# Hybrid attention and pooling block: pooled-branch loads and latents moved earlier, last output product in two halves

## The chip, the cores and the metric

The kernel runs on one core of a Trainium2 chip. The metric is device microseconds of one execution. A core has TensorE (PE in the profile, its weight loads PEld), VectorE (DVE), ScalarE (ACT), GpSimd (POOL) and SyncE (SP), each with a queue of its own that it works through in order. SP issues nearly all transfers of this kernel.

## The reference

One layer over 1024 tokens of width 1024. One input projection makes the latents of attention, two SiLU gates, the input of a pooling branch and the merge gates. Both branches are gated, projected and merged; an output projection, a residual add and a normalisation of each row end it.

```python
hn = rms_norm(h, norm_in)
zq, zkv, zkr, g_attn, u_pool, g_pool, g_merge = split(hn @ w_in)
y_attn = mla_attention(zq, zkv, zkr, ...) * silu(g_attn)     # 8 heads, chunk-causal
y_pool = multiscale_pool(u_pool, ...) * silu(g_pool)         # windows 2, 4, 8, 16
a = y_attn @ w_branch_attn
p = y_pool @ w_branch_pool
gate_a, gate_p = split(sigmoid(g_merge))
h = h + (gate_a * a + gate_p * p) @ w_out
return rms_norm(h, norm_final)
```

## The kernel before

Every fp32 operand is split into a high and a low part (`split`: ACT casts the high part, DVE subtracts it to get the low part), and a product is three matmuls: high by high, high by low, low by high. Tiles are 128 rows high; a matmul writes up to 512 columns of a PSUM bank.

The order of the work is not that of the source. Each helper (`mms`, `act`, `tt`, `dma`, ...) adds an `Op` to a `Plan`. `Plan.order` then schedules all of them with one running time per engine and a modelled cost of each operation: of the operations whose inputs are there, an engine takes the earliest in program order among those that could start within 30 of the first (line 189). Tiles come from tags with a fixed number of slots (`SLOTS`, line 25): 45 slots of `t`, one of `wr` (raw weights), two each of `wh` and `wl` (their high and low parts), two banks pairs `s` (scores) and one bank `f` (products of the pooled branch) among them. The result is one fixed queue for each engine. An instruction whose input is late holds up all that stand behind it in its queue.

The program has these stages.

1. **Input projection**: pairs of column blocks in seven products each instead of eight (`Pair`). `gate_pair(14, ...)` is the last; beside its products 4 and 6 stand the two `Latents` items (line 1148), which load the q and kv latents (`zq`, `zkv`) again, normalise and split them.
2. **Up products** (`run_up`): q and k of all heads from the latents, results written to DRAM by head (`qn_d`, `kn_d`). The first q item also loads the four pooled rows `yp` (`y<-y_d`); each k item splits one of them (lines 830 to 831). `run_rope` makes the rotary part of q. Weights: `w_uq`, `w_uk`, `w_uv`.
3. **Value products** (`run_v`): eight products `pv`, each with a cast on ACT and a subtraction on DVE.
4. **Attention**: eight heads. Head h loads the rows of head h+1 (`load_head`: `qh`, `ql`, `kh`, `kl`), and one tile `mp[h]` of the pooled branch's merge gates (lines 1412 to 1413). Then scores `sc`, their maximum on DVE, the exponential on ACT (`pr`), transposes `pt`, their split `pT`, and the product with the values `o`. Score banks have two slots, so a score waits until the exponential two before it has read its slot.
5. **Pooled-branch products** (`run_branch_p`, eight items of 24 matmuls, `pf`) lie between the matmuls of the heads. Each needs its weights (`wr<-w_bp`, split to `wh` and `wl`) and, at the end of each half, multiplies the bank into `mp[t]`. There is one bank for them, so the next half waits for that multiplication.
6. **Branch items** (`BranchItem`): the attention branch's projection, merge, and the loads of the blocks of `w_out` (`BLOCKS`).
7. **Output projection**: `Ahead` and four `OutPair`s, each with six products of two row tiles; `Rows` adds the products onto the residual rows, squares and sums them, scales by the final norm (`nf`) and by the reciprocal root, and writes out. The pair i = 3 is the last.

Of the kernel before, what the change touches and what calls it, by code (L numbers as in the profile page):

```python
# [209 lines left out]
def hybrid_block_kernel(  # L210
# [30 lines left out]
    def buf(tag, cols, dt, name):  # L241
        uid[0] += 1
        nm = f"{name}_{uid[0]}"
        pool = pp if tag in PSUM else tp
        b = Buf(lambda: pool.tile([P, cols], dt, tag=tag, bufs=SLOTS[tag], name=nm), tag)
        b.nm = name
        return View(b, 0, P, 0, cols)
# [9 lines left out]
    def t32(name):  # L257
        return buf("t", T, F32, name)
# [45 lines left out]
    def tt(o, a, b, op, eng="DVE"):  # L304
        e = nc.vector if eng == "DVE" else nc.gpsimd
        c = 1.055 * a.n + 145 if eng == "DVE" else 2.2 * a.n + 150
        port = eng == "POOL" or not (psum(a) or psum(b))
        plan.add(eng, lambda: e.tensor_tensor(real(o), real(a), real(b), op), c, [a, b], [o], port=port)  # L308
# [16 lines left out]
    def stt(o, a, s, b, op0, op1):  # L325
        c = 1.055 * a.n + 145 + 62 * len(views(s))
        plan.add(
            "DVE",
            lambda: nc.vector.scalar_tensor_tensor(real(o), real(a), real(s), real(b), op0, op1),
            c,  # L330
            views(a, s, b),
            [o],
            port=not (psum(a) or psum(b)),
        )
# [37 lines left out]
    def dma(o, x, late=None):  # L372

        v = o if isinstance(o, View) else x
        p0, p1, c0, c1 = v.box
        plan.add(
            "SP",
            lambda: nc.sync.dma_start(real(o), real(x)),  # L378
            450,
            views(x, late),  # L380
            views(o),
            (p1 - p0) * (c1 - c0) * 4,
        )
# [18 lines left out]
    def split_tile(x):  # L402
        h, l = tr("hi"), tr("lo")
        split(h, l, x)
        return h, l
# [55 lines left out]
    def cell(n=1):  # L461
        a = small_at[0]
        small_at[0] += n
        return small[:, a : a + n]
# [340 lines left out]
    def load_rope(h):  # L805
        d = heads[h % 2]
        j = 32 * (h % 4)
        for x, n in enumerate("hl"):
            dma(d["q" + n][64:96, :].f32(), qr_d[h // 4][x][j : j + 32, :])
# [9 lines left out]
    def run_up(p, which, first):  # L819
        def run(it):  # L820
            acc = next_acc()
            cs = state["cq"] if which == "q" else state["ckv"]
            n = len(cs)
            if first:
                shared[which] = (it.h, it.l)
            if which == "q" and p == 0:
                for g in range(4):
                    yp[g] = t32("y")
                    dma(yp[g], y_d[g])
            if which == "k":  # L830
                yp[p] = split_tile(yp[p])
            if which == "k" and p == 1:
                dress_slots(heads[0])
                load_rope(0)
            wh, wl = shared[which]
            o = n * (p if which == "k" else p % 2)
            prod(acc, wh[o : o + n], wl[o : o + n], halves(cs))
            h, l = tr("uh"), tr("ul")
            for ps, a, b in acc.spans:
                split(h[:, a:b], l[:, a:b], ps)  # L840
            dst = qn_d if which == "q" else kn_d
            if p == 0:
                if which == "q":
                    make_slots()
                dma(heads[0][which + "h"][0:64, :].f32(), h[0:64, :].f32())
                dma(heads[0][which + "l"][0:64, :].f32(), l[0:64, :].f32())
            r = 64 if p == 0 else 0
            dma(dst[p][0][r:P, :], h[r:P, :].f32())
            dma(dst[p][1][r:P, :], l[r:P, :].f32())
        return run  # L850
# [22 lines left out]
    def run_v(j):  # L873
        def run(it):
            if j == 0:
                shared["v"] = (it.h, it.l)
            wh, wl = shared["v"]
            c = "pofp"[j % 4]
            ps = buf(c, 512, F32, "pv")
            sl = slice(128 * j, 128 * j + 128)  # L880
            seq = []
            for k, (ch, cl) in enumerate(state["ckv"]):
                seq += [(ch[:, sl], wh[k]), (ch[:, sl], wl[k]), (cl[:, sl], wh[k])]
            mms([(ps, a, b, n == 0, n == 5) for n, (a, b) in enumerate(seq)])
            v = tr("v")
            v4 = lambda x: v.via(
                lambda a: a.rearrange("p (h x d) -> p h x d", h=HEADS, x=2)[:, :, x, :]
            )
            pv = ps.via(lambda a: a.rearrange("p (h d) -> p h d", h=HEADS))
            acopy(v4(0), pv)  # L890
            tt(v4(1), pv, v4(0).f32(), ALU.subtract)
            vt.append(v)
        return run

    yp = [None] * 4
# [230 lines left out]
    def gate_pair(t, beside=()):  # L1126
        items.append(Pair(14 + t, (spill_sigmoid(gate_d[t]), spill_sigmoid(gate_d[t + 1])), beside))
# [17 lines left out]
    silu_pair(4, ga_d[2:4])  # L1145
    gate_pair(10)
    gate_pair(12, [(3, Rotary())])
    gate_pair(14, [(4, q), (6, kv)])
    for n, it in enumerate(i for i in items if isinstance(i, Pair)):
        for j, f in enumerate(hooks.get(n, [])):  # L1150
            it.after[1 + 3 * j] = f
# [11 lines left out]
    n_pre = len(items)  # L1163

    mp = [None] * 8

    def rows_of(t):
        return m_d[t // 4][128 * (t % 4) : 128 * (t % 4) + 128, :]
# [22 lines left out]

    ys = []

    BLOCKS = ("b11", "b21", "t2", "t1", "t3", "b22", "t4")
    blocks_at = {
        "b11": (w_top, 0),
        "b21": (w_low, 0),
# [5 lines left out]
    class BranchItem(Item):  # L1203
# [7 lines left out]
        def load(self):  # L1211
            super().load()
            self.g = t32("gate")
            dma(self.g, gate_d[self.t])
            self.blocks = []
            for n in BLOCKS[self.t : self.t + 1]:
                src, c = blocks_at[n]
                for j in range(2):
                    raw = t32("wo")
                    k2 = lambda a: a.rearrange("(k p) c -> p k c", p=P)  # L1220
                    x = src[256 * j : 256 * j + 256, c : c + 512]
                    dma(raw.via(lambda a: a.rearrange("p (k c) -> p k c", k=2)), x.via(k2) if isinstance(x, View) else k2(x))
                    self.blocks += [raw[:, lft], raw[:, rgt]]
# [26 lines left out]
    class Rows:  # L1250


        def __init__(self, i):
            self.row = [i, i + 4]
            self.t = [t32("res"), t32("res")]
            self.ss = [cell(2), cell(2)]
            self.st = [cell(), cell()]
            for e in range(2):
                dma(self.t[e], xr[128 * self.row[e] : 128 * self.row[e] + 128, :])

        def add(self, e, h, bank):
            v = self.t[e][:, (lft, rgt)[h]]
            tt(v, bank, v, ALU.add)

        def square(self, e, h):
            act(buf("go", 512, F32, "junk"), self.t[e][:, (lft, rgt)[h]], AF.Square, acc=self.ss[e][:, h : h + 1])
# [4 lines left out]

        def finish(self, e, last=False):
            r, ss, st = self.t[e], self.ss[e], self.st[e]
            tt(st, ss[:, 0:1], ss[:, 1:2], ALU.add)
            act(st, st, AF.Sqrt, scale=1.0 / D, bias=eps)
            recip(st, st)
            o = out[128 * self.row[e] : 128 * self.row[e] + 128, :]
            if last:
                act(r[:, rgt], r[:, rgt], AF.Copy, scale=st)
                stt(r[:, lft], r[:, lft], st, nf[:, lft], ALU.mult, ALU.mult)  # L1280
            else:
                stt(r, r, st, nf, ALU.mult, ALU.mult)
            for c in (lft, rgt):
                dma(o[:, c], r[:, c])
# [32 lines left out]
    class OutPair(Pair):  # L1317
# [30 lines left out]
        def run(self, it, tick):  # L1348
            i, R = self.i, self.rows
            b = first["b"][i]  # L1350
            c = first["c"][i] or buf("of"[i - 2], 512, F32, "pb")
            a = buf("p", 512, F32, "pb")
            tick()
            R.add(0, 0, b)
            self.product(a, 1, True)
            R.add(0, 0, a)
            R.square(0, 0)
            tick()
            self.product(b, 2, False)
            R.add(0, 1, b)  # L1360
            tick()
            self.product(c, 3, True)
            R.add(1, 1, c)
            tick()
            self.product(b, 4, False)
            R.add(1, 1, b)
            R.square(1, 1)
            if i == 3:
                R.scale(1, 1)
            tick()  # L1370
            self.product(c, 5, False)
            R.add(0, 1, c)
            R.square(0, 1)
            R.finish(0)
            tick()
            self.product(b, 6, False)
            R.add(1, 0, b)
            R.square(1, 0)
            R.finish(1, i == 3)

    raw_tag[0] = "t"
    for t in range(8):
# [24 lines left out]
    for h in range(HEADS):  # L1407
        if h + 1 < HEADS:
            load_head(h + 1)
        if 0 < h < 4:  # L1410
            load_gate(h)
        mp[h] = t32("mp")
        dma(mp[h], gate_d[8 + h])
        s = heads[h % 2]
        for qr in range(4):
            prs = []
# [139 lines left out]
```

## Time and profile before

| what | us |
|---|---|
| median of 3 runs | 705.21 (702.76 to 706.47) |
| profiled execution | 705.3 |
| its span | 703.4 |

The profiled execution is 0.1 above the median of the runs, and its span leaves 1.9 around it. PE is busy for 97% of the span. A row of the timeline gives the start of an instruction, its duration, engine, line, operation and tiles, and in brackets how long the engine had been idle before it and what ended that. `sc`, `pf`, `pv`, `pt` and `o` are PSUM tiles of the products named above, `ps` and `pb` those of the input and output projections.

### The profile page before, as it was taken

Reading aid. Unit: us, or ns where it says so; the run is one execution under the profiler, and the core shown is the slowest. Engines: PE = TensorE matmul, PEld = TensorE weight load, DVE = VectorE, ACT = ScalarE, POOL = GpSimd, SP = SyncE. Lnnn points to the kernel's source line nnn. Section 1 sums busy time; section 2 is a strip of 40 time slices with the busy share of each in tenths; the row PEclk is TensorE's granted clock in tenths of the full one; section 3 lists DMA queues with packets and bytes.
Section 4 is the critical chain, followed back from the end, with each engine's and each line's share of the span. In section 5 each row is a group of like instructions: output and inputs, shape, how many; then the busy total and the mean of one; then the engine's idle time right before and its main releaser. Section 6 shows DMA issues by size and latency. Waiting matters only on the chain.

```text
span 703.4 us, 9678 instructions
## 1 busy us (share of the span) xinstructions
PE 681.5 (97%) x3356; PEld 573.3 (82%) x3356; DVE 539.8 (77%) x863; ACT 355.8 (51%) x657; POOL 115.6 (16%) x153
## 2 busy tenths in 40 slices
PE   8999999999999999999998879999999999999995
PEld 6878888888888888888886769999998978878884
DVE  5698996768878577768869548878787899957883
ACT  6854535442444354444436537677666673425431
POOL 0020100400022030400101023445454200000000
PEclk9999999999999999999999989999999999999999
DMA  8956666452977549375687973454441399784522
GB/s 317 377 189 253 210 221 179 99 160 102 308 211 180 179 162 298 101 180 156 243 278 276 332 165 107 110 145 121 106 120 46 108 378 336 227 258 160 187 83 89
DMA packets 55871, 136.42 MB, mean 194 GB/s; under 512 B 5904, under 2 KB 17296, under 8 KB 55696
## 3 DMA queue, kind: packets, MB, share of 16 engines
q1 hardware_dynamic: 53568, 131.63, 56.0%
q0 software_dynamic: 2256, 4.20, 4.3%
q8 instruction: 26, 0.43, 0.3%
q14 instruction: 21, 0.17, 0.1%
HBM read 93.73 MB, written 46.27 MB: 199 GB/s over the span
## 4 chain that ended last, share of the span: by engine, by line
PE 84%; DMA 6%; DVE 5%; ACT 2%; issue 1%; SPq 1%; DVEq 0%; ACTq 0%
PE pb L275 33%; PE ps L275 30%; PE sc L275 6%; PE pf L275 6%; PE o L275 4%; PE pt L282 4%; DMA mp<-gate_d 2%; DMA m_d<-gate 1%; DMA kl<-kr_d 1%; DVE lo L308 1%; DMA wr<-w_uv 1%; DVE ra L308 1%; DVE gate L308 1%; SPq L378 1%; DMA wr<-w_bp 1%
## 5 line engine op out<-in xcount | busy, mean ns | idle before, releaser
L275 PE MATMUL pb<-t,wp 128*128 128x512 f32 x504 | 120.9, 389 | 0.0
L275 PEld LDWEIGHTS pb<-t,wp 128*128 128x128 f32 x504 | 94.6, 188 | 19.6
L298 ACT CAST wp<-wr 128x512 fp32r<-128x512 f32 x98 | 59.4, 620 | 93.3 <-PE ps L275 53.1
L308 DVE TENSOR_TENSOR wp<-wr,wp 128x512 fp32r<-128x512 f32 x98 | 72.0, 748 | 36.8 <-ACT wp L298 35.5
L275 PE MATMUL ps<-xa,wp 128*128 128x512 f32 x224 | 74.0, 390 | 0.0
L322 POOL TENSOR_SCALAR pr<-pr,small 128x384 f32<-128x384 f32 (+4 forms) x64 | 48.2, 759 | 73.8 <-DVE small L348 65.9
L308 DVE TENSOR_TENSOR pT<-pt,pT 128x512 fp32r<-128x512 f32 (+1 forms) x80 | 48.4, 632 | 12.1 <-ACT pT L298 11.8
L290 ACT ACTIVATE pr<-sc,small 128x384 f32<-128x384 f32 (+4 forms) x64 | 47.6, 745 | 18.8 <-DVE small L357 17.7
L298 ACT CAST pT<-pt 128x512 fp32r<-128x512 f32 (+1 forms) x80 | 41.5, 545 | 29.8 <-PE pt L282 29.0
L357 DVE TENSOR_REDUCE small<-sc 128x1 f32<-128x128 f32 (+3 forms) x64 | 47.6, 751 | 10.4 <-PE sc L275 10.0
L275 PEld LDWEIGHTS ps<-xa,wp 128*128 128x128 f32 x224 | 42.0, 188 | 8.7
L275 PE MATMUL o<-pT,v 128*128 128x256 f32 (+1 forms) x320 | 47.8, 281 | 0.2 <-DVE pT L308 0.2
L275 PEld LDWEIGHTS o<-pT,v 128*128 128x128 f32 x320 | 44.4, 189 | 3.3 <-DVE pT L308 0.4
L275 PE MATMUL ps<-xb,wp 128*128 128x512 f32 x112 | 43.6, 389 | 0.0
L282 PE MATMUL pt<-ident,pr 128*128 128x128 f32 x288 | 42.7, 278 | 0.0
L275 PE MATMUL ps<-t,wp 128*128 128x512 f32 x168 | 40.8, 390 | 0.0
L275 PE MATMUL pb<-xa,wp 128*128 128x512 f32 x168 | 40.7, 389 | 0.0
L275 PE MATMUL pb<-wo,wp 128*128 128x512 f32 x168 | 39.9, 389 | 0.0
L275 PE MATMUL sc<-kh,qh 128*128 128x384 f32 (+4 forms) x96 | 36.2, 377 | 2.3 <-ACT pr L290 2.3
L275 PEld LDWEIGHTS pb<-wo,wp 128*128 128x128 f32 x168 | 31.5, 188 | 6.6
L275 PEld LDWEIGHTS pb<-xa,wp 128*128 128x128 f32 x168 | 31.5, 188 | 6.5
L275 PEld LDWEIGHTS ps<-t,wp 128*128 128x128 f32 x168 | 31.4, 188 | 6.5
(206 smaller groups left out, 1444.9 us busy)
## 6 DMA issues: line engine op xcount, KB each, us to landing
wr<-w_z SPq DMA_DIRECT2D x30, 512.0 KB, 5.2
gate_d<-z SPq DMA_DIRECT2D x16, 512.0 KB, 3.4
xt<-xr SPq DMA_DIRECT2D x8, 512.0 KB, 10.5
mp<-gate_d SPq DMA_DIRECT2D x8, 512.0 KB, 5.0
gate<-gate_d SPq DMA_DIRECT2D x8, 512.0 KB, 5.8
wo<-wt_d SPq DMA_DIRECT2D x8, 512.0 KB, 8.7
m_d<-gate SPq DMA_DIRECT2D x16, 256.0 KB, 4.2
mr<-m_d SPq DMA_DIRECT2D x16, 256.0 KB, 4.4
```

The source lines that it names most:

```text
L275: nc.tensor.matmul(real(o), real(a), real(b), start=s, stop=e, **kw)
L282: nc.tensor.transpose(real(o), real(a), real(ident))
L290: nc.scalar.activation(real(o), real(x), func, scale=real(scale), **kw)
L298: lambda: nc.scalar.copy(real(o), real(x)),
L308: plan.add(eng, lambda: e.tensor_tensor(real(o), real(a), real(b), op), c, [a, b], [o], port=port)
L322: e.tensor_scalar(real(o), real(a), real(s1), real(s2), op0, op1)
L357: lambda: nc.vector.tensor_reduce(real(o), real(a), axis=AX.X, op=ALU.max, negate=True),
L378: lambda: nc.sync.dma_start(real(o), real(x)),
```

## The change

Four edits.

- **Gates fetched with the pooled rows.** `mp[0]` is loaded in the first q item, right behind the pooled rows, `mp[1]` in the second k item. Heads 2 to 7 load theirs as before.
- **Latents one product sooner.** They stand beside products 3 and 5 of the last pair instead of 4 and 6.
- **Pooled rows split between value products.** The four `split_tile(yp[p])` move from the four k items to value products 0, 2, 4 and 6.
- **Last product in two halves.** In the last `OutPair`, product 1 (A12 by b21) is computed last, in two banks of 256 columns. The second row tile (e = 1) is finished ahead of it; the first is added, scaled and squared in pieces of 256. A `None` in `BLOCKS` moves the loads of the block `t4` one branch item later.

```diff
-            if which == "k":
-                yp[p] = split_tile(yp[p])
+                load_mp(0)
             if which == "k" and p == 1:
...
+                load_mp(1)
...
             vt.append(v)
+            if j in (0, 2, 4, 6):
+                p = (0, 2, 4, 6).index(j)
+                yp[p] = split_tile(yp[p])
...
-    gate_pair(14, [(4, q), (6, kv)])
+    gate_pair(14, [(3, q), (5, kv)])
...
+    def load_mp(t):
+        mp[t] = t32("mp")
+        dma(mp[t], gate_d[8 + t])
...
-    BLOCKS = ("b11", "b21", "t2", "t1", "t3", "b22", "t4")
+    BLOCKS = ("b11", "b21", "t2", "t1", "t3", "b22", None, "t4")
...
+        def piece(self, bank, n):
+            c = slice(256 * n, 256 * n + 256)
+            v, ss = self.t[0][:, c], self.ss[0]
+            tt(v, bank, v, ALU.add)
+            act(buf("go", 512, F32, "junk")[:, :256], v, AF.Square, acc=ss[:, 2 * n : 2 * n + 1])
+            if n == 0:
+                tt(ss[:, 0:1], ss[:, 0:1], ss[:, 1:2], ALU.add)
+                tt(v, v, nf[:, c], ALU.mult)
...
-            if last:
+            if last and not e:
                 act(r[:, rgt], r[:, rgt], AF.Copy, scale=st)
-                stt(r[:, lft], r[:, lft], st, nf[:, lft], ALU.mult, ALU.mult)
+                stt(r[:, 256:512], r[:, 256:512], st, nf[:, 256:512], ALU.mult, ALU.mult)
+                ts(r[:, :256], r[:, :256], st, None, ALU.mult)
+            elif last:
+                act(r, r, AF.Copy, scale=st)
...
-        mp[h] = t32("mp")
-        dma(mp[h], gate_d[8 + h])
+        if h > 1:
+            load_mp(h)
...
+            R.scale(1, 0)
+            R.finish(1, True)
+            for n in range(2):
+                q = slice(256 * n, 256 * n + 256)
+                a = buf("p", 512, F32, "pb")[:, :256]
+...
+                R.piece(a, n)
+            R.finish(0, True)
```

The queue of ACT in the second half of head 0, before. A number behind a name tells tiles of one name apart; `pr<-sc` are the exponentials of 768 and 896 keys and of head 1's first block.

```order
L298 CAST pT_3403<-pt_3390 128x384
L290 ACTIVATE pr_3317,small<-sc_3374,small 128x768
L290 ACTIVATE pr_3311,small<-sc_3397,small 128x896
L298 COPY oa_3438<-o_3411 64x256
L298 CAST pT_3452<-pt_3440 128x512
L298 CAST pT_3465<-pt_3446 128x512
L290 ACTIVATE pr_3311,small<-sc_3455,small 128x128
L298 CAST pT_3492<-pt_3483 128x384
L290 ACTIVATE pr_3498,small<-sc_3417,small 128x1024
L290 ACTIVATE pr_3317,small<-sc_3494,small 128x256
L298 COPY oa_3516<-o_3477 64x256
L298 CAST wh_3525<-wr_3352 128x512
```

The same stretch of ACT now.

```order
L298 CAST pT_3422<-pt_3403 128x384
L290 ACTIVATE pr_3325,small<-sc_3392,small 128x768
L298 CAST wh_3434<-wr_3359 128x512
L298 COPY oa_3453<-o_3438 64x256
L290 ACTIVATE pr_3323,small<-sc_3418,small 128x896
L298 CAST pT_3476<-pt_3462 128x512
L298 CAST pT_3488<-pt_3468 128x512
L298 CAST pT_3509<-pt_3497 128x384
L290 ACTIVATE pr_3517,small<-sc_3449,small 128x1024
L290 ACTIVATE pr_3323,small<-sc_3479,small 128x128
```

The cast of the third pooled weights (`wh<-wr`, the last row before, the third now) has moved ahead of the copy and the exponential of 896 keys. The weights' load on SP, before, behind the last loads of head 1's rows:

```order
L378 DMA ql_3289<-qn_d_2944 64x1024
L378 DMA kl_3291<-kn_d_3136 64x1024
L378 DMA mp_3309<-gate_d_2255 128x1024
L378 DMA wr_3352<-w_bp 128x512
L378 DMA qh_2916<-qr_d_3001 32x1024
```

The same place of SP now.

```order
L378 DMA kh_3291<-kn_d_3113 64x1024
L378 DMA ql_3293<-qn_d_2962 64x1024
L378 DMA kl_3295<-kn_d_3141 64x1024
L378 DMA wr_3359<-w_bp 128x512
L378 DMA qh_2928<-qr_d_3013 32x1024
```

The load of `mp[0]` is gone from between; it stands 48 places further up, behind the pooled rows. On PE, 15 pooled matmuls `pf` stand ahead of head 1's first score before, and 30 now. On DVE the last rows of the program, before (`res_6104` is the second row tile, `res_6102` the first):

```order
L308 TENSOR_TENSOR res_6102<-pb_6288,res_6102 128x512
L308 TENSOR_TENSOR small<-small 128x1
L348 RECIPROCAL small<-small 128x1
L329 SCALAR_TENSOR_TENSOR res_6102<-res_6102,small,nf_5696 128x1024
L308 TENSOR_TENSOR res_6104<-ps_5837,res_6104 128x512
L308 TENSOR_TENSOR small<-small 128x1
L348 RECIPROCAL small<-small 128x1
L329 SCALAR_TENSOR_TENSOR res_6104<-res_6104,small,nf_5696 128x512
```

The same end of DVE now.

```order
L308 TENSOR_TENSOR res_6104<-ps_5801,res_6104 128x512
L308 TENSOR_TENSOR res_6102<-pb_6189,res_6102 128x256
L308 TENSOR_TENSOR res_6104<-res_6104,nf_5701 128x512
L308 TENSOR_TENSOR small<-small 128x1 x2
L308 TENSOR_TENSOR res_6102<-res_6102,nf_5701 128x256
L348 RECIPROCAL small<-small 128x1
L308 TENSOR_TENSOR res_6102<-pb_6352,res_6102 128x256
L308 TENSOR_TENSOR small<-small 128x1
L348 RECIPROCAL small<-small 128x1
L329 SCALAR_TENSOR_TENSOR res_6102<-res_6102,small,nf_5701 128x256
L320 TENSOR_SCALAR res_6102<-res_6102,small 128x256
```

The wide last operation of the first row tile is gone from the end, the finish of the second stands among the pieces of the first, and the add of the second piece (`pb_6352`) stands behind the reciprocal of the second tile.

## Rows read from the trace of the kernel before

**Rows 1.** The page: busy time of each engine, share of the span, instructions.

```profile
PE 681.5 (97%) x3356; PEld 573.3 (82%) x3356; DVE 539.8 (77%) x863; ACT 355.8 (51%) x657; POOL 115.6 (16%) x153
```

**Rows 2.** Timeline of PE, the idle times between 370 and 420 us.

```profile
373.34 0.73 PE L275 MATMUL ps<-hi,wl 128*128 128x512 f32 x2 [1.37 <-DVE wl L308]
...
385.02 0.50 PE L275 MATMUL pv<-wh,hi 128*128 128x512 f32 x1 [1.41 <-DVE ul L308]
...
403.32 0.41 PE L275 MATMUL sc<-kh,qh 128*128 128x320 f32 x1 [1.48 <-ACT pr L290]
...
415.49 0.80 PE L275 MATMUL pf<-hi,wh 128*128 128x512 f32 x1 [4.87 <-DVE mp L308]
...
418.50 0.46 PE L275 MATMUL sc<-kh,qh 128*128 128x128 f32 x1
```

**Rows 3.** Timeline of ACT, SP and DVE, 400 to 416 us.

```profile
401.70 0.62 ACT L298 CAST wh<-wr 128x512 fp32r<-128x512 f32 x1 [2.65 <-DMA wr<-w_bp]
...
402.35 0.69 DVE L308 TENSOR_TENSOR wl<-wr,wh 128x512 fp32r<-128x512 f32 x1 [1.49 <-ACT wh L298]
...
403.44 0.59 SPq L378 DMA_DIRECT2D kl<-kn_d  x1
...
404.09 0.57 SPq L378 DMA_DIRECT2D mp<-gate_d  x1
...
406.51 0.36 SPq L378 DMA_DIRECT2D wr<-w_bp  x1
...
409.46 1.01 ACT L290 ACTIVATE pr<-sc,small 128x896 f32<-128x896 f32 x1 [1.01 <-DVE small L348]
...
414.74 0.69 DVE L308 TENSOR_TENSOR mp<-pf,mp 128x512 f32<-128x512 f32 x1 [5.30 <-DMA mp<-gate_d]
```

**Rows 4.** Transfers issued from 403.4 to 406.8 us: size, us from issue to landing.

```profile
mp<-gate_d SPq DMA_DIRECT2D x1, 512.0 KB, 10.6
kl<-kn_d SPq DMA_DIRECT2D x1, 256.0 KB, 9.3
wr<-w_bp SPq DMA_DIRECT2D x1, 256.0 KB, 9.5
```

**Rows 5.** Stretches: sum; PE, PEld, DVE, ACT, POOL busy; clock; DMA share, GB/s.

```profile
376.00:410.00 34.00, 30.75 (x151) 25.29 (x150) 25.06 (x40) 20.77 (x39) 5.02 (x8) 1.00 1.01 324
414.45:421.25 6.80, 5.76 (x20) 4.97 (x21) 3.77 (x8) 1.63 (x4) 1.90 (x3) 0.53 0.46 94
421.35:424.00 2.65, 2.65 (x21) 2.48 (x21) 0.95 (x3) 1.58 (x4) 0.09 (x1) 1.00 0.00 0
```

**Rows 6.** Lines by form: count, busy, mean ns; value subtractions and pooled-row subtractions on DVE.

```profile
L308 DVE TENSOR_TENSOR v<-pv,v 128x512 fp32r<-128x512 f32 x8 | 5.3, 685 | 2.5 <-ACT v L298 2.5
...
L308 DVE TENSOR_TENSOR lo<-y,hi 128x1024 fp32r<-128x1024 f32 x4 | 4.9, 1215 | 0.0
```

**Rows 7.** Timeline of the end of the program.

```profile
692.79 2.88 PE L275 MATMUL ps<-wo,wp 128*128 128x512 f32 x12
...
695.26 1.28 DVE L329 SCALAR_TENSOR_TENSOR res<-res,small,nf 128x1024 f32<-128x1024 f32 x1
...
696.46 0.68 DVE L308 TENSOR_TENSOR res<-ps,res 128x512 f32<-128x512 f32 x1
...
697.24 0.63 ACT L290 ACTIVATE junk<-res 128x512 f32<-128x512 f32 x1 [2.21 <-DVE res L308]
...
698.18 0.29 ACT L290 ACTIVATE small<-small,eps 128x1 f32<-128x1 f32 x1 [0.23 <-DVE small L308]
...
698.71 0.72 ACT L290 ACTIVATE res<-res,small 128x512 f32<-128x512 f32 x1 [0.23 <-DVE small L348]
```

**Rows 8.** By form and from PE's timeline: rows nearest to the new shapes.

```profile
L308 DVE TENSOR_TENSOR oa<-o,oa 64x256 f32<-64x256 f32 x32 | 13.4, 419 | 3.5 <-ACT oa L298 3.0
...
L290 ACT ACTIVATE z<-z 128x1024 f32<-128x1024 f32 x16 | 16.7, 1058 | 16.1 <-DVE z L308 16.1
...
553.71 1.14 PE L275 MATMUL o<-pT,v 128*128 128x256 f32 x8
```

More of the change, by code (lines that the diff above doesn't have):

```diff
@@ L1215, in load @@
             self.blocks = []
-            for n in BLOCKS[self.t : self.t + 1]:
+            for n in filter(None, BLOCKS[self.t : self.t + 1]):
                 src, c = blocks_at[n]
@@ L1255, in __init__ @@
             self.t = [t32("res"), t32("res")]
-            self.ss = [cell(2), cell(2)]
+            self.ss = [cell(3), cell(2)]
             self.st = [cell(), cell()]
@@ L1273, in finish @@
             r, ss, st = self.t[e], self.ss[e], self.st[e]
-            tt(st, ss[:, 0:1], ss[:, 1:2], ALU.add)
+            if last and not e:
+                tt(st, ss[:, 0:1], ss[:, 2:3], ALU.add)
+            else:
+                tt(st, ss[:, 0:1], ss[:, 1:2], ALU.add)
             act(st, st, AF.Sqrt, scale=1.0 / D, bias=eps)
@@ L1277, in finish @@
             o = out[128 * self.row[e] : 128 * self.row[e] + 128, :]
-            if last:
+            if last and not e:
                 act(r[:, rgt], r[:, rgt], AF.Copy, scale=st)
-                stt(r[:, lft], r[:, lft], st, nf[:, lft], ALU.mult, ALU.mult)
+                stt(r[:, 256:512], r[:, 256:512], st, nf[:, 256:512], ALU.mult, ALU.mult)
+                ts(r[:, :256], r[:, :256], st, None, ALU.mult)
+            elif last:
+                act(r, r, AF.Copy, scale=st)
             else:
@@ L1351, in run @@
             c = first["c"][i] or buf("of"[i - 2], 512, F32, "pb")
-            a = buf("p", 512, F32, "pb")
+            last = i == 3
             tick()
             R.add(0, 0, b)
[L1355 to L1358, printed above, removed]
+            if not last:
+                a = buf("p", 512, F32, "pb")
+                self.product(a, 1, True)
+                R.add(0, 0, a)
+                R.square(0, 0)
+                tick()
             self.product(b, 2, False)
@@ L1367, in run @@
             R.square(1, 1)
-            if i == 3:
+            if last:
                 R.scale(1, 1)
@@ L1373, in run @@
             R.square(0, 1)
-            R.finish(0)
+            if last:
+                R.scale(0, 1)
+            else:
+                R.finish(0)
             tick()
@@ L1378, in run @@
             R.square(1, 0)
-            R.finish(1, i == 3)
+            if not last:
+                R.finish(1)
+                return
+            R.scale(1, 0)
[3 more added lines that the diff above has]
+                a = buf("p", 512, F32, "pb")[:, :256]
+                for k, ((ah, al), (bh, bl)) in enumerate(zip(self.ops["A12"], W["b21"])):
+                    mms(
+                        [
+                            (a, ah, bh[:, q], k == 0, False),
+                            (a, ah, bl[:, q], False, False),
+                            (a, al, bh[:, q], False, k == 3),
+                        ]
+                    )
+                R.piece(a, n)
+            R.finish(0, True)
     raw_tag[0] = "t"
```

## The prediction

> **What bounds the kernel now.** The page's first part comes first: PE is busy for 681.5 of 703.4 us, DVE for 539.8 [rows 1]. What can be won on PE is the time in which it stands, the time at the lower clock, and the tail. So I next read PE's timeline for idle times. Around the places of the change it stands four times: 1.37 at 373.3 and 1.41 at 385.0, both for DVE's low parts, 1.48 at 403.3 for an exponential, 4.87 at 415.5 for DVE's multiplication into `mp` [rows 2]. The timeline of the other engines says why. DVE waited 5.30 for the gate tile, issued at 404.09; ACT stood 2.65 for the second pooled weights, ahead of the exponential for which PE stood 1.48 [rows 3]. The transfers say why those are late: the gate tile lands 10.6 after its issue, at 414.7, and from 376 to 410 the DMA engines are busy all the time (share 1.01) [rows 4, 5]. Transfers land in the order of issue: head 1's last rows at 403.44 + 9.3 = 412.7, the gates at 414.7, the third pooled weights at 406.51 + 9.5 = 416.0 [rows 3, 4]. The long wait costs twice: from 414.45 to 421.25 the granted clock is 0.53 (1.2 of 2.4 GHz), and 5.76 us of PE work lie there, which lose 0.47 x 5.76 = 2.7; behind, it is 1.00 again [rows 5].
>
> **Loads of the gates.** The wait for `mp` goes: tile 0 is now issued behind the pooled rows, tile 1 in the k items, long before their use. What is late next stands in the queue of ACT: the cast of the third pooled weights has moved ahead of the exponential of 896 keys, which in the profile ran at 409.46 without waiting for a transfer [rows 3]. Head 1's first score needs the bank that this exponential reads. So PE's wait for DVE becomes a wait for ACT, and ACT's is one for the third weights. When do these land? Before, at 416.0; ahead of them the 512 KB of gates no longer stand, which took 414.7 - 412.7 = 2.0. That makes 414.0. The load of tile 1 now stands further up in the busy stretch, but `w_uv` has left that stretch for the idle engines ahead of it, and I set one against the other. Bounds: 412.0, if the queue gains another 2.0 in that exchange, and 416.0, if it gains nothing.
>
> From there: cast 0.62, the copy ahead of the exponential 0.42 (nearest row: DVE's addition on the same shape, 419 ns [rows 8]), exponential 1.01 [rows 3], two hand-overs of about 0.1. The score starts at 416.25, where before it started at 418.50 [rows 2]: 2.25 less. By then 30 pooled matmuls are done and not 15. One costs 2.72 / 12 = 0.227, 2.88 being the time of twelve with the last one's overlap of 0.16 [rows 7]. Fifteen make 3.4 us that PE needn't do later, and they would run at full clock. Together 5.65.
>
> The clock takes some back. PE would arrive at the score at: 415.49 - 4.87 = 410.6, plus half of the 3.0 from 415.49 to 418.50 (which ran at half clock) = 412.1, minus the three smaller waits (4.26), plus fifteen products (3.4), plus about 1.0 for the first softmax of head 0 (below) = 412.3. It then waits 4.0. Before, it had stood 3.8 us, from 410.6 to 414.45, when the lower clock came [rows 2, 5], so the fall is likely again, with its loss of 2.7 now wholly behind the score. Before, only 421.25 - 418.50 = 2.75 lay behind it, a loss of 1.3. So +1.4 (0 less 1.3 if the clock just holds).
>
> **Latents, and pooled rows between value products.** These take the first three waits away: the latents are split a product sooner, and `w_uk` is issued five places earlier; DVE's subtractions of 1.215 each leave the k items, where a low part was late by 1.41 [rows 2, 6]; and the second weights no longer stand behind all of the k writes. What they add: the value phase has 48 matmuls x 0.227 = 10.9 us of PE, and DVE now has 8 x 0.685 + 4 x 1.215 = 10.3 in it [rows 6]. It fits, with nothing to spare, so head 0's first maximum can come late: 0 to 2, I take 1.0. By themselves these edits are worth nothing in the forecast: all that PE gains here, it gives back at the score that waits for the third weights. They count only if that wait is short.
>
> **The tail.** Before, the last product's matmuls run to 695.67 (692.79 + 2.88), and the last scale ends at 699.43: 3.76 us [rows 7]. The 0.68 of the addition had first waited for a wide operation of 1.28 (it ended 696.54). Now the halves. Two times twelve matmuls of 256 columns: eight took 1.14 [rows 8], with the overlap of 0.16 that is 0.12 each, 24 make 2.9 against 2.72: +0.2. Behind the last one the work is shorter, but two queues have something ahead of it. On DVE the second piece's addition stands behind the first piece's multiplication (0.42 [rows 8]) and the reciprocal of the second tile, whose chain (squares 0.63, small steps 0.16 to 0.29, hand-overs 0.23 [rows 7]) starts only when product 6 is added; I get the addition's end 1.7 behind PE's. On ACT the copy over the whole second tile, 1.06 [rows 8], stands ahead of the second piece's square: it ends at 2.4. Square 0.47, sum, root, reciprocal 0.84 and hand-overs: 3.75. Scale of 512 columns 0.72: 4.5, against 3.76. So +0.7, with the +0.2 makes **+0.9**. Bounds: -1.4, if neither queue holds the piece up (the wait behind 1.28 gone, addition and square a third shorter), and +1.5, if the second tile's chain is later by its 0.6 of hand-overs.
>
> The Trainium skill, "TensorE: Matmul & The Clock Gate", section "Back-to-back issue gap", has sustained spacings of 81 ns at 128 columns and 131 at 512; an estimate between them, some 98 ns, makes 24 halves 2.35 us and the sum about 0.5 lower. The rows disagree already at 512, with 227 ns and not 131 [rows 7], so I don't use it.
>
> **The load of `t4`** goes into a later branch item. That stretch is PE-bound with the load hidden; nothing, with bounds of -0.5 and +0.5. The pooled products left behind the last score are 48 and not 60 (the order of PE); they cover DVE and ACT at the end of attention: 0, bounds -1 and +1.
>
> **Sum.** 705.3 - 5.65 + 1.4 + 0.9 = 701.95, and 0.1 less since the profiled execution lies 0.1 above the median: **701.9**.
>
> **Rivals.**
> *A, the forecast.* The wait moves to the third weights. With the clock falling 701.9; with it just holding 701.9 - 2.7 = 699.2. For it: the cast's place in ACT's queue, and landings in the order of issue. [...] Own range 699.2 to 703.2.
> *B, the third weights are early*, by 412.0 or sooner. Then PE meets the score with 0 to 2 of a wait (score at 412.3 to 414.2), and the clock holds: (418.50 - 412.3) + 3.4 + 1.3 = 10.9 at best, 9.0 at worst, with the tail +0.9: 695.2 to 697.1. For it: all small waits are gone and the slot for raw weights comes free sooner. Against it: the engines are full from 376 on, and PE's gain doesn't make bytes land sooner.
> The Trainium skill, "DMA: Bandwidth & Descriptors", section "Queues, rings and completion order", says that completion is "not FIFO per issuing engine": by that the third weights could land ahead of head 1's rows, and B would hold. The rows show landings at 412.7, 414.7, 416.0, in the order of issue [rows 3, 4], which speaks against it.
> *C, the change doesn't do what it says.* The weights still land at 416.0, since tile 1 and the earlier loads fill the gap that tile 0 left. Score at 418.25, gain 0.25 + 3.4, less 1.4 and 0.9: 703.9.
> *D, slower.* The slot of the raw weights is one; it comes free when DVE has subtracted the second weights, and DVE now carries 4.9 us more in the value phase. If that delays the third weights' issue, all of head 1 moves: 1 us for each us of landing behind 414.0. From 417.3 on the kernel is as now, and from 420.8 on it is slower by 3.5. For it: DVE's 10.3 of 10.9. Against it: DVE ended that subtraction at 403.0, 3.5 ahead of the issue [rows 3].
>
> **How the numbers follow.** A 0.51, B 0.27, C 0.16, D 0.06. 0.5% is 3.5 us, about what a measurement can tell from no change: faster is below 701.7. B is faster, and half of A (0.24): 0.51. C and the other half of A are the same: 0.43. D: 0.06. The range goes from 696.0, in the middle of B, to 704.8, above C with 0.9 for the unknown end of attention.
>
> **What would show it.** In the profile of the changed kernel: no idle time of PE for DVE's low parts near 373 and 385, and none for `mp`; a cast `wh<-wr` on ACT that waits several us for the transfer `wr<-w_bp`; a score `sc` on PE that waits 3 to 5 us for ACT at about 416, with the granted clock near 0.5 behind it; from PE's end to the span's end 8.4, where it is 7.7 now. I am wrong if the cast doesn't wait (B), if the weights land at 416 or later (C, D), or if the tail is shorter than before.

## The result and the profile after

| | before | after |
|---|---|---|
| median of 20 runs, us | 705.29 (702.76 to 709.68) | 701.88 (700.03 to 704.61) |
| ratio to before | | 0.9949, 95% interval 0.9935 to 0.9963 |
| profiled execution, its span | 705.3, 703.4 | 702.37, 700.2 |

The kernel became about 0.5% faster, by the amount forecast. Whether by the way forecast is read from the same views. First the page's busy times: PE has as much to do as before [rows 1].

```profile
PE 682.6 (97%) x3368; PEld 574.3 (82%) x3368; DVE 539.6 (77%) x868; ACT 355.9 (51%) x660; POOL 116.8 (17%) x153
```

PE's timeline, 380 to 420 us; in brackets the idle time before and what ended it.

```profile
395.20 0.50 PE L275 MATMUL pf<-hi,wh 128*128 128x512 f32 x1 [0.28 <-DVE v L308]
...
404.04 0.38 PE L275 MATMUL o<-pT,v 128*128 128x256 f32 x1 [1.53 <-ACT pT L298]
404.86 0.90 PE L275 MATMUL o<-pT,v 128*128 128x256 f32 x3 [0.43 <-DVE pT L308]
...
417.40 0.33 PE L275 MATMUL sc<-kh,qh 128*128 128x128 f32 x1 [1.97 <-ACT pr L290]
```

Of the waits in [rows 2] none is left; together with one of 0.37 (at 398.64) they were 9.50 from 370 to 420, and now there are 4.21. The two longest of the new ones, 1.53 and 1.97, end at ACT. ACT's timeline says what it did meanwhile.

```profile
402.99 0.62 ACT L298 CAST wh<-wr 128x512 fp32r<-128x512 f32 x1 [4.93 <-DMA wr<-w_bp]
...
415.22 0.62 ACT L298 CAST wh<-wr 128x512 fp32r<-128x512 f32 x1 [3.55 <-DMA wr<-w_bp]
...
416.25 1.01 ACT L290 ACTIVATE pr<-sc,small 128x896 f32<-128x896 f32 x1
```

It stood 4.93 for the second pooled weights and 3.55 for the third, with a transposed block's cast (`pT`) and the exponential of 896 keys queued behind them. In [rows 3] the same exponential ran at 409.46. The transfers issued from 403.4 to 408.1 (KB, us to landing):

```profile
kl<-kn_d SPq DMA_DIRECT2D x1, 256.0 KB, 7.8
wr<-w_bp SPq DMA_DIRECT2D x1, 256.0 KB, 7.6
```

The third weights landed at 415.14, where it was 416.0 before [rows 4]. Of the stretches at a lower clock there are two (columns as in [rows 5]).

```profile
404.10:408.20 4.10, 3.67 (x14) 3.41 (x15) 2.64 (x7) 1.50 (x5) 1.27 (x2) 0.58 0.80 213
418.35:421.80 3.45, 3.45 (x14) 2.96 (x13) 2.94 (x6) 0.98 (x2) 0.51 (x1) 0.51 1.04 202
```

They lose 0.42 x 3.67 + 0.49 x 3.45 = 3.2, and the one stretch before lost 2.7. The end of the program, from the timeline:

```profile
690.21 1.95 PE L275 MATMUL pb<-wo,wp 128*128 128x256 f32 x15
...
693.08 0.17 DVE L348 RECIPROCAL small<-small 128x1 f32<-128x1 f32 x1
693.16 0.41 DVE L308 TENSOR_TENSOR res<-pb,res 128x256 f32<-128x256 f32 x1
...
693.28 1.15 ACT L290 ACTIVATE res<-res,small 128x1024 f32<-128x1024 f32 x1 [0.23 <-DVE small L348]
694.34 0.40 ACT L290 ACTIVATE junk<-res 128x256 f32<-128x256 f32 x1
...
695.99 0.35 DVE L320 TENSOR_SCALAR res<-res,small 128x256 f32<-128x256 f32 x1
```

The other nine of the 24 halves stand earlier in PE's queue, near 667 and 682. From the last matmul (692.16) to the last scale (696.34) it is 4.18, where it was 3.76 [rows 7]. The last addition starts 1.0 behind PE and right behind the reciprocal; the last square starts when the wide copy of 1.15 ends. The whole end, from a wait that both kernels have (the start of this row) to the span's end, grew from 703.4 - 633.27 = 70.13 to 700.2 - 629.06 = 71.14. Before:

```profile
633.27 1.20 PE L275 MATMUL ps<-wo,wp 128*128 128x512 f32 x4 [0.61 <-DVE wp L308]
```

After:

```profile
629.06 1.19 PE L275 MATMUL ps<-wo,wp 128*128 128x512 f32 x4 [0.61 <-DVE wp L308]
```

The program's start differs too. PE's first products with `xb`, before and after:

```profile
6.43 0.73 PE L275 MATMUL ps<-xb,wqh 128*128 128x512 f32 x2 [0.31 <-ACT xb L290]
```

```profile
7.85 0.73 PE L275 MATMUL ps<-xb,wqh 128*128 128x512 f32 x2 [1.29 <-ACT xb L290]
```

So the account of the two profiled executions: waits from 370 to 420 less 5.3, clock +0.5, end +1.0, start +1.4, waits between 420 and 600 less 0.9. That makes -3.3, and the spans differ by 3.2. The start isn't the change's doing: this wait for `xb` runs from under 0.2 to 1.29 in the fourteen profiles of this study, and in experiment 3, which begins with the same program as the changed kernel, it is under 0.2.

### The profile page after: what moved, and what is told of

It reads as the page before. It is cut to its first block, busy times and chain, and to the rows that moved or that the text cites. A ratio compares the mean times of both kernels' runs of the same rounds, so it can differ in the third digit from the quotient of the medians.

```text
span 700.2 us, 9698 instructions
## 1 busy us (share of the span) xinstructions
PE 682.6 (97%) x3368; PEld 574.3 (82%) x3368; DVE 539.6 (77%) x868; ACT 355.9 (51%) x660; POOL 116.8 (17%) x153
## 4 chain that ended last, share of the span: by engine, by line
PE 88%; DMA 4%; DVE 3%; issue 2%; ACT 1%; SPq 1%; DVEq 0%; ACTq 0%
PE pb L275 36%; PE ps L275 31%; PE sc L275 6%; PE pf L275 5%; PE o L275 5%; PE pt L282 4%; PE pv L275 2%; DMA kh<-kr_d 1%; DMA wr<-w_bp 1%; SPq L378 1%; DMA x<-xT 1%; DVE mr L308 1%; DMA mr<-m_d 1%; DVE small L357 0%; DVE res L308 0%
## 5 line engine op out<-in xcount | busy, mean ns | idle before, releaser
L322 POOL TENSOR_SCALAR pr<-pr,small 128x128 f32<-128x128 f32 (+3 forms) x64 | 48.7, 765 | 77.3 <-DVE small L348 68.9
L290 ACT ACTIVATE pr<-sc,small 128x128 f32<-128x128 f32 (+3 forms) x64 | 47.6, 745 | 19.3 <-DVE small L357 16.4
L275 PE MATMUL pb<-wo,wp 128*128 128x512 f32 (+1 forms) x180 | 40.5, 376 | 0.2 <-DVE res L308 0.2
```

What stands on the lines that cost most here:

```text
L275: nc.tensor.matmul(real(o), real(a), real(b), start=s, stop=e, **kw)
L290: nc.scalar.activation(real(o), real(x), func, scale=real(scale), **kw)
L322: e.tensor_scalar(real(o), real(a), real(s1), real(s2), op0, op1)
```

## The experiments

Times are medians; a ratio is to runs of the kernel before that were taken with them, with its 95% interval. The changed kernel has 0.9949 (0.9935 to 0.9963). Each diff shows the lines that matter, and `...` marks lines left out.

**1. The gates alone.** The kernel before with the early loads of the two gate tiles and nothing else.

```diff
+                load_mp(0)
...
+                load_mp(1)
...
-        mp[h] = t32("mp")
-        dma(mp[h], gate_d[8 + h])
+        if h > 1:
+            load_mp(h)
```

> The kernel before with one of the four edits: the two gate tiles loaded early. Theory (the gain comes from taking the late gate tile off PE's path): the wait of 4.87 us and its half clock go, the two smaller waits near 373 and 385 stay (2.8); in ACT's queue the third pooled weights stand behind the exponential of 896 keys here, so PE meets head 1's rows (landing at 412.7 before) instead: 699 to 702 us. Rival (the gates alone only swap one late transfer for the next, and the gain needs the latents and the moved splits): 703.5 to 705.5.

698.36, ratio 0.9891 (0.9862 to 0.9920): a little below the range of the theory, and one edit of four is faster than all four. ACT, then PE, of this run:

```profile
409.39 1.01 ACT L290 ACTIVATE pr<-sc,small 128x896 f32<-128x896 f32 x1
414.62 0.62 ACT L298 CAST wh<-wr 128x512 fp32r<-128x512 f32 x1 [3.17 <-PE pf L275]
```

```profile
412.94 0.33 PE L275 MATMUL sc<-kl,qh 128*128 128x128 f32 x1 [1.61 <-DMA kl<-kn_d]
```

The exponential runs ahead of the third cast, and in this stretch PE waits for head 1's rows only, 1.61; the clock stays at 1.00 from 400 to 424. The other three edits thus cost 3.5 together by the medians, 4.1 by the ratios.

**2. The casts later.** The changed kernel; the planner is told that two loads take longer.

```diff
+LAG = 6000.0
...
-                op.end = dma_at + 930
+                op.end = dma_at + 930 + op.lag
...
+        items[-1].lag = LAG if t in (1, 2) else 0.0
```

The items t = 1 and t = 2 load the second and the third pooled weights.

> The changed kernel, with the planner told that the loads of the second and third pooled weights take 6 us longer than it reckons. It then puts their casts on ACT behind the exponentials and casts that PE waits for at 404.0 and 417.4. Theory (PE stands because late weights block ACT's queue): both waits (1.53 + 0.43 and 1.97) shrink and with them the stretches at half clock: 1.5 to 5 us faster than the changed kernel, 697 to 700.4. Rival (the transfers are the bound, and PE only meets the same weights or head 1's rows a little later): within 1 us of 701.9.

698.26, 0.9890 (0.9856 to 0.9924), as the theory had it. The waits at 404.0 and 417.4 are gone, and PE waits for head 1's rows instead:

```profile
412.86 0.33 PE L277 MATMUL sc<-kl,qh 128*128 128x128 f32 x1 [1.96 <-DMA wr<-w_bp]
```

The rows landed at 412.82; the transfer that the profile names landed later, at 414.05. Behind this wait the clock is lower for a while (0.71 from 412 to 416).

**3. The end undone.** The changed kernel with the old `Rows`, last pair and `BLOCKS`.

> The changed kernel with the last pair, its rows and the order of the w_out blocks as before. Theory (the halves cost more than they save: in the changed profile the last scale ends 4.18 us behind the last matmul, 3.76 before, and the halves take 0.2 more): 0.3 to 0.9 faster than the changed kernel, seen at the end of the profile as 7.7 from PE's end to the span's end in place of 8.04. Rival (the shorter last operations help): 0.5 to 1.4 slower.

702.48, 0.9943 (0.9924 to 0.9961): not to be told from the changed kernel, where 0.3 to 0.9 less was expected. The profile tells more: its end is 701.2 - 631.08 = 70.12, against 71.14, so the halves do cost 1.0. But the old order of `BLOCKS` is back as well, and ahead of the end PE now stands where it doesn't in the changed kernel:

```profile
613.70 0.61 PE L275 MATMUL ps<-wo,wm 128*128 128x512 f32 x2
...
625.90 3.29 PE L275 MATMUL pb<-wo,wp 128*128 128x512 f32 x12 [0.38 <-ACT wp L298]
629.67 0.73 PE L275 MATMUL ps<-wo,wp 128*128 128x512 f32 x2 [0.48 <-ACT wp L298]
```

From the first of these products with the blocks of `w_out` to the wait at 631.08 it is 17.4, where the changed kernel takes 15.1 (614.01 to 629.06). The other runs agree: 16.9 to 18.0 with the old order (experiments 1, 8, 11), 14.1 to 16.5 with the new one (the other eight). The kernel before, which gets there later (618.11), takes 15.2 with the old order. So the later load of `t4`, the one of the two edits that bears on this stretch, gives back what the halves cost; no run has one of the two without the other.

Up to the loads of `w_out`, near 595, this is the changed kernel's program, in another execution:

```profile
415.85 0.47 PE L275 MATMUL sc<-kh,qh 128*128 128x128 f32 x1 [5.71 <-DMA ql<-qn_d]
```

```profile
398.87 0.62 ACT L298 CAST wh<-wr 128x512 fp32r<-128x512 f32 x1 [2.17 <-DMA wr<-w_bp]
413.66 0.62 ACT L298 CAST wh<-wr 128x512 fp32r<-128x512 f32 x1 [7.29 <-DMA wr<-w_bp]
414.70 1.01 ACT L290 ACTIVATE pr<-sc,small 128x896 f32<-128x896 f32 x1
```

Here the second weights came at 398.84 and not at 402.97, PE wasn't held at 404, and all of the waiting, 5.71, lies at head 1's first score. It is ended by the exponential (414.70 + 1.01 = 415.71); the transfer that the profile names had landed at 411.37.

**4. Products 5 and 6 exchanged** in the last pair.

```diff
-            self.product(c, 5, False)
...
+            if not last:
+                self.product(c, 5, False)
...
             self.product(b, 6, False)
...
             R.finish(1, True)
+            tick()
+            self.product(c, 5, False)
+            R.add(0, 1, c)
+            R.square(0, 1)
+            R.scale(0, 1)
```

> The changed kernel with products 5 and 6 of the last pair exchanged, so that the second row tile is complete 2.7 us sooner and its wide copy on ACT (1.15) and the reciprocal ahead of the last addition on DVE needn't stand between the pieces. Theory (the tail is held by what stands ahead in the two queues): from the last matmul's end to the last scale 2.8 to 3.4 us instead of 4.18, the run 0.8 to 1.3 faster. Rival (the chain add, square, root, reciprocal, scale sets it by itself): within 0.3 of the changed kernel's 4.18.

700.82, 0.9923 (0.9898 to 0.9949): by the intervals not to be told from the changed kernel. From the last matmul to the last scale it is 3.70 in place of 4.18 (693.56 to 697.26), where 2.8 to 3.4 was expected. The second tile's sum stood on DVE behind an addition and a multiplication for the first tile (0.69 and 0.68), so that the wide copy still ran ahead of the last square:

```profile
694.21 1.15 ACT L290 ACTIVATE res<-res,small 128x1024 f32<-128x1024 f32 x1
...
695.26 0.40 ACT L290 ACTIVATE junk<-res 128x256 f32<-128x256 f32 x1
```

The size was wrong, the mechanism is half confirmed.

**5. The splits back in the k items**, all else as changed.

```diff
+            if which == "k":
+                yp[p] = split_tile(yp[p])
...
-            if j in (0, 2, 4, 6):
-                p = (0, 2, 4, 6).index(j)
-                yp[p] = split_tile(yp[p])
```

> The changed kernel with the four splits of the pooled rows back in the k items (gates early, latents sooner and the halves stay). ACT's queue has the third pooled weights' cast behind the exponential of 896 keys again. Theory (the moved splits put that cast ahead, and that is what the changed kernel pays): no wait of PE for ACT at head 1's first score, 697.5 to 700. Rival (the sooner latents are what costs): 701 to 703.

698.64, 0.9908 (0.9877 to 0.9939). There is no wait for ACT at head 1's score; PE waits for head 1's rows, and 1.51 for DVE at the value products again:

```profile
411.89 0.33 PE L275 MATMUL sc<-kl,qh 128*128 128x128 f32 x1 [1.84 <-DMA kl<-kn_d]
```

The moved splits are what cost. They also change the order of PE, with 18 pooled matmuls ahead of that score and not 30; experiments 9 and 10 hold that fixed.

**6. The latents at 4 and 6 again**, all else as changed.

```diff
-    gate_pair(14, [(3, q), (5, kv)])
+    gate_pair(14, [(4, q), (6, kv)])
```

> The changed kernel with the latents beside products 4 and 6 again (gates early, splits between value products and the halves stay). In ACT's queue the second pooled weights' cast stands ahead of the exponential of 896 keys, the third behind it and behind head 1's first exponential. Theory (what counts is which exponential stands behind a late cast): the wait moves to the second weights, which land some 10 us sooner, so it is short: 699 to 702, with the wait for DVE's low part near 373 back (1.4). Rival (the moved splits cost by themselves, DVE being full in the value phase): 702 to 705.

710.39, 1.0071 (1.0045 to 1.0097): slower than before, and outside both expected ranges. PE at the first pooled products, and after the last head:

```profile
398.41 0.50 PE L275 MATMUL pf<-hi,wh 128*128 128x512 f32 x1 [1.63 <-DVE v L308]
400.38 0.80 PE L275 MATMUL pf<-hi,wl 128*128 128x512 f32 x1 [1.24 <-DVE wl L308]
...
564.43 0.50 PE L275 MATMUL pf<-hi,wh 128*128 128x512 f32 x1 [2.02 <-DVE mp L308]
568.23 0.50 PE L275 MATMUL pf<-hi,wh 128*128 128x512 f32 x1 [0.78 <-DVE mp L308]
572.14 0.47 PE L275 MATMUL pf<-hi,wh 128*128 128x512 f32 x1 [0.88 <-DVE mp L308]
```

Values and weights come late by 2.9, with a lower clock for a while (0.73 from 396 to 404). The queues of ACT and DVE show what stood ahead of them:

```profile
395.93 0.62 ACT L298 CAST wh<-wr 128x512 fp32r<-128x512 f32 x1 [1.79 <-DMA wr<-w_bp]
396.46 1.07 ACT L298 CAST v<-pv 128x512 fp32r<-128x512 f32 x2
```

```profile
397.07 1.29 DVE L308 TENSOR_TENSOR v<-pv,v 128x512 fp32r<-128x512 f32 x2 [1.25 <-ACT v L298]
398.50 1.23 DVE L308 TENSOR_TENSOR lo<-y,hi 128x1024 fp32r<-128x1024 f32 x1
399.65 0.68 DVE L308 TENSOR_TENSOR wl<-wr,wh 128x512 fp32r<-128x512 f32 x1
```

Again ACT stood for weights, here the first pooled ones, with the casts of two values queued behind; DVE waited for those, and then had the split of a pooled row ahead of the weights' low part. The first weights were issued at 389.27 and landed at 395.86; in the changed kernel they had landed at 378.80, ahead of the value products. Later there are 75 pooled matmuls left after the last score (48 in the changed kernel), where each half waits for the one bank (3.7). I have not accounted for the rest of its 8.5.

**7. Casts later, and only the first gate tile early.** As 2, with the second tile loaded at head 1.

```diff
-                load_mp(1)
-        if h > 1:
+        if h > 0:
             load_mp(h)
```

> The second experiment (casts later) with only the first gate tile early; the second is loaded at head 1 as before. Its 512 KB no longer stand ahead of head 1's rows. Theory (head 1's rows, in a full stretch of transfers, are what PE meets once the casts are out of the way): the rows land 1.5 to 2 us sooner, PE's wait of 1.96 at 412.9 and its half clock go: 695 to 697.5. Rival (the wait comes back at the second tile, which now lands late for head 1): 698 to 701.

697.88, 0.9903 (0.9877 to 0.9928). Head 1's rows land at 410.28 and not at 412.82, the third weights at 410.75 and not at 414.05; the wait and the lower clock are gone. But small waits appear for ACT (0.71 at 398.16), POOL and DVE (0.29, 0.60, 0.50 from 417 to 425), and the total, between the two expected ranges, is that of 2 within the intervals.

**8. Only the first gate tile, on the kernel before.** The edit of 1 without `load_mp(1)`.

> The kernel before with only the first gate tile loaded early. Theory: as the first experiment (698.4), less its wait of 1.61 for head 1's rows, since the second tile's 512 KB are out of the full stretch: 696 to 698. The second pooled weights' cast stands ahead of an exponential here, as before (wait 1.48 at 403.3), which takes up to 1.5 back. Rival: the second tile comes late and PE waits for it at head 1, 699 to 702.

697.60, 0.9895 (0.9869 to 0.9920): as 1, by the total. The wait for head 1's rows is gone, the one of 1.56 at 403.45 for the second cast is back.

**9. The third cast alone later**, and **10. the second alone**: experiment 2 in halves.

```diff
+LAG = 6000.0
...
+        items[-1].lag = LAG if t == 2 else 0.0
```

That is 9; in 10 it is `t == 1`.

> The changed kernel with the longer load told to the planner for the third pooled weights alone: ACT's queue is the changed kernel's up to the exponential of 768 keys; the third cast moves from there to behind head 1's second exponential, and 30 pooled matmuls stand ahead of head 1's first score as in the changed kernel. Theory (that one cast is the cost of the moved splits): 697.5 to 699.5, as in the second experiment (698.3); PE meets head 1's rows instead. Rival (the second cast costs as much): 700 to 702.

> The other half: the longer load told for the second pooled weights alone. Their cast moves behind the exponentials of 384 and 512 keys; the third cast still stands ahead of the exponential of 896 keys. Theory: the score of head 1 still waits for the third weights' cast, 701 to 703. Rival (the second cast is what costs): 697.5 to 700.

9: 698.52, 0.9903 (0.9878 to 0.9928). 10: 702.32, 0.9958 (0.9938 to 0.9978). In 9 PE, with the exponential at 410.34, waits 1.07 at head 1:

```profile
413.69 0.33 PE L277 MATMUL sc<-kl,qh 128*128 128x128 f32 x1 [1.07 <-DMA kl<-kn_d]
```

In 10 the cast of the third weights still holds ACT, and PE stands longest of all:

```profile
417.04 0.48 PE L277 MATMUL sc<-kh,qh 128*128 128x128 f32 x1 [6.44 <-DMA ql<-qn_d]
```

```profile
414.85 0.62 ACT L300 CAST wh<-wr 128x512 fp32r<-128x512 f32 x1 [8.26 <-DMA wr<-w_bp]
415.89 1.01 ACT L292 ACTIVATE pr<-sc,small 128x896 f32<-128x896 f32 x1
```

Both have 30 pooled matmuls ahead of the score, like the changed kernel, and up to that score ACT's queue in 9 is the changed kernel's without the third cast. So the place of this one cast is worth the 3.8 between them. That is a net figure: the planner orders what follows differently too, and in 9 (as in 2, not in 10) PE later stands at the first product behind the pooled ones, with the clock at 0.66 from 566 to 571.

```profile
567.21 1.22 PE L277 MATMUL ps<-hi,wl 128*128 128x512 f32 x2 [2.26 <-DVE wl L310]
```

**11. What the runs pointed to**: first gate tile early, latents sooner, splits in the k items, the old end, and 2 us more told to the planner for `w_bp[1]` and `w_bp[2]`.

> What the runs so far point to: only the first gate tile early, the latents sooner, the splits of the pooled rows in the k items, the end of the program as before, and the second and third pooled weights' casts behind the exponentials (the planner told 2 us more for their loads). Theory: as the fifth experiment (698.6) less its wait of 1.84 for head 1's rows, less some 1.5 of its half clock and less 0.5 of the tail: 694 to 696.5. Rival (these gains are lost to the wait for the second tile or to the end of attention): 697 to 699.

697.14, 0.9870 (0.9843 to 0.9897). The fastest, faster than the changed kernel by the intervals, yet not to be told from 1, 2, 7, 8 and 9; it lies in the range of the rival (697 to 699), above that of the theory. The span of its profiled execution is 694.9. PE waits 0.63 for head 1's rows and keeps the clock:

```profile
410.47 0.33 PE L277 MATMUL sc<-kl,qh 128*128 128x128 f32 x1 [0.63 <-DMA kl<-kn_d]
...
620.41 3.32 PE L277 MATMUL pb<-wo,wp 128*128 128x512 f32 x12 [1.47 <-ACT wp L300]
```

The second row is a wait of 1.47 that is 0.27 in experiment 1; it takes part of the gain back, and it lies in the stretch that the old order of `BLOCKS`, which this run has, makes longer (experiment 3).

**12. Scales on GpSimd** in the last pair of the changed kernel.

```diff
-            tt(v, v, nf[:, (lft, rgt)[h]], ALU.mult)
+            tt(v, v, nf[:, (lft, rgt)[h]], ALU.mult, "POOL")
```

> The changed kernel with the three 512-wide multiplications by the final norm in the last pair on GpSimd instead of DVE. Theory (the last addition comes 1.0 late because DVE's queue is full of them): from the last matmul's end to the last scale 3.4 to 3.8 us in place of 4.18. Rival (ACT's wide copy over the second tile holds the last square in any case, and it needs the scaled tile): 4.0 to 5.0. The total changes by under 1 us either way, 701 to 703.

702.04, 0.9946 (0.9929 to 0.9964). From the last matmul to the last scale 3.45 (697.19 to 700.64), in place of 4.18: with the multiplications off DVE the last addition starts 0.04 behind PE, and the last square runs before the wide copy.

```profile
697.23 0.42 DVE L308 TENSOR_TENSOR res<-pb,res 128x256 f32<-128x256 f32 x1
...
698.33 1.15 ACT L290 ACTIVATE res<-res,small 128x1024 f32<-128x1024 f32 x1
698.57 0.15 DVE L308 TENSOR_TENSOR small<-small 128x1 f32<-128x1 f32 x1
699.38 0.28 ACT L290 ACTIVATE small<-small,eps 128x1 f32<-128x1 f32 x1
```

So DVE's queue held the last addition. The wide copy still costs something: the last sum is there at 698.72, and the root that needs it starts at 699.38, when the copy ends.

## Why the prediction was right, step by step

**The forecast mechanism is shown.** The wait for the gate tile went, and PE's wait became one for ACT, which stood for the third pooled weights. Experiments 9 and 10 tie it to that cast: with it alone moved the kernel takes 698.52, with the other alone 702.32.

**Landing of the third weights: 414.0 forecast, 415.14 measured**; 413.58, 416.14 and 419.71 in experiments 3, 4 and 12, which are the same program up to there. Two of the four lie outside the bounds of 412.0 to 416.0, but the executions were apart already at the first pooled product (395.20 in the changed kernel's profile; 393.84, 396.64 and 399.16), so most of the spread isn't the queue's. That the second gate tile and `w_uv` cancel is not shown: the tile alone is worth 3.3 (410.75 without it, 414.05 with it, experiments 7 and 2), and no run has `w_uv`'s part. From the landing to the score it is 2.26 or 2.27 in all four, for the 2.25 added up in the forecast. In the profiled execution the term of 5.65 is thus about 1 too large.

**The wait of 4.0 and the clock.** In the profiled execution the wait is 1.97, since PE had lost 1.96 at 404 for the second weights. I had said that these no longer stand behind all of the writes; they landed at 402.97, later than the 401.62 of before. In experiments 3, 4 and 12 PE wasn't held there, and the score waited 5.71, 5.45 and 6.32, longer than forecast: PE came to the score further ahead of the landing than I had reckoned (3.4 in experiment 3, for 1.7). That moves no time as long as the landing sets the score. The clock's loss was put at 2.7 behind the score; it is 3.2 in two stretches, the first behind the wait at 404. Rival B had the clock hold after a wait of up to 2; here it fell after 1.97.

**"By themselves these edits are worth nothing": wrong.** I took the latents and the moved splits for harmless and wrote the cast's place down to the whole change. The moved splits bring the cast ahead (experiment 5 against the changed kernel: -3.2). Without them the change would have been worth 6.6 us (705.2 to 698.64) and not 3.4. Sooner latents, together with the new end, are worth nothing measurable with the splits where they were (experiments 1 and 5), and save 8.5 where the splits are moved (experiment 6).

**The end: +0.9 forecast, +1.0 measured** (71.14 against 70.13), but of other parts. Behind the last matmul +0.7 was forecast and the last scale comes 0.4 later (4.18 for 3.76); to the span's end it is 8.0, for the 8.4 forecast. PE itself reaches its last matmul 0.7 later, of which the halves explain the forecast 0.2. Most of the rest is a wait for DVE that the forecast didn't have: the three matmuls from 650.50 make 0.68, and the next starts 1.07 behind them.

```profile
650.50 0.87 PE L275 MATMUL pb<-wo,wp 128*128 128x512 f32 x3
651.57 3.01 PE L275 MATMUL pb<-wo,wp 128*128 128x512 f32 x12 [0.20 <-DVE res L308]
```

The two queues named do hold the end behind the last matmul; experiment 12 took DVE's part away and with it 0.73. The load of `t4` was put at nothing, within 0.5; next to experiment 3, which gets to the blocks of `w_out` at the same time with the old order, it is worth 2.3.

**The sum was right in part by luck**: a landing one later, a start of the program 1.4 slower in this execution, and 0.9 fewer waits in attention offset each other, and so did the two misses in the end.

**The rivals.** B (weights by 412.0) held in none of these four executions. The Trainium skill, "DMA: Bandwidth & Descriptors", section "Queues, rings and completion order", allows a later transfer to complete first; its example is a transfer on one DMA engine behind one on sixteen. In all fourteen profiles SP's transfers landed in the order of issue, so no run here shows it. C (weights at 416.0) lies within the spread of landings, as experiment 4 has it, and can't be held apart from A by the time. D named the right place, the value phase, but the kernel got slower there only with the late latents of experiment 6. There DVE was busy for 9.9 of the 14 us from 384 to 398 and itself stood 1.25 for ACT, which stood for weights.

## What to carry to other kernels

Where a planner writes fixed queues, ask of each instruction that waits for a load what stands behind it: a cast of weights that no one needs yet held the exponential for which TensorE stood, because the planner reckoned the load faster than the 7.6 to 10.0 us that these two loads took in the full stretch. Telling the planner the longer time was worth as much as the three other edits had cost. And test the parts of a change one by one: here one of four carried more than the whole.

## What was not expected of the hardware

The same load in the same program took from 7.3 to 10.0 us. The second weights were issued at 392.93 and landed at 402.97 in the changed kernel's profile; in experiments 3, 4 and 12 it was 391.17 to 398.84, 394.14 to 401.48 and 395.93 to 404.67. PE's wait moved with that from one place to another while the time stayed: from the first pooled product to the product at 629.06 (in experiment 4 at 630.51) it is 233.9 in both executions, with the wait split in the one and whole in the other.

The clock fell after short waits too: after 1.97 at 417.4 it was 0.51 from 418.35 to 421.80, with PE at work; after 1.61 in experiment 1 and 1.07 in experiment 9 it stayed at 1.00. And the same wait of 2.26 for the same low part (`wl`, at 567.21 in experiment 9, at 567.89 in experiment 2) stands beside 0.66 from 566 to 571 in the one and 1.00 in the other.
